# Branch B's gates in seven-product pairs, and branch B's projection beside the mLSTM

## The chip, the cores and the metric

The kernel runs on one core of one Trainium2 chip. The metric is the device time in microseconds of one launch. Before the change it is 1658.83 us, the median of 3 runs (1658.51 to 1659.03).

## The reference

One layer of a block with two branches, over S = 1024 positions and D = 1024 channels, in fp32. Both branches and both gates are cut out of one projection of the normed input; the branches are projected, gated, added, projected once more and added to the input.

```
h = rmsnorm(x, norm_g)
(a_q, a_k, a_v, a_o, a_z, a_g, b_q, b_k, b_v, b_z, g_a, g_b) = split(h @ w_in)
y_a = rmsnorm(mlstm(silu(conv(a_q, a_k)), a_v, a_g)) * sigmoid(a_o) * silu(a_z)   # both directions, 4 heads
y_b = rmsnorm(diff_attention(rope(b_q), rope(b_k), b_v)) * silu(b_z)              # 8 heads
mix = sigmoid(g_a + gate_b[0]) * (y_a @ w_branch_a) + sigmoid(g_b + gate_b[1]) * (y_b @ w_branch_b)
out = rmsnorm(x + mix @ w_out, final_g)
```

## The kernel before

All products run in fp32 by parts: each operand is split into a high part H and a low part L (`fp32r` tiles), and a product is three matmuls, wH·rH, wH·rL and wL·rH. A weight block of 1024×128 is loaded as `raw` (512 KB), cast to wH by ACT (L231) and subtracted to wL by POOL (L239, or in eight slices at L237). A projection of 128 outputs (`proj`, L565, matmuls L579) is two halves of 512 positions, each 8 blocks of k × 3 = 24 matmuls of 128x512; it is given out in eight pieces of three.

The stages, by the profile: an opening with norm and transposes; two wide pairs for a_v; sixteen pairs (a_k, a_q with their convolution, a_o, a_z) in which two blocks of 128 outputs together take seven half-size products in place of eight (`pair_units`, L355), 7×12 = 84 matmuls of 128x512 where two plain projections take 96; the differential attention, head by head; the mLSTM; the mixing; the output.

A pair's sink turns its sums into results and writes them to DRAM (`oz_sink`, L462; `conv_sink`, L492). The last product of a result stays in PSUM and one to three earlier ones come out of SBUF copies, so a sink gets a PSUM tile and a `rest` to add.

The sixteen gate projections (eight of g_b, then eight of g_a; `gate_units`, L984) are plain projections with a tanh on ACT (L993) and a store of the result. They are the *other work* that fills PE between dependent steps: five run in the attention's last part, eleven in the mLSTM, where `ml_units` (L1411) deals out their pieces by a table (`share`): three pieces before this step, two after that one.

After the mLSTM the mixing reads y_b from DRAM row by row (`load_y`, L1484: load of 512 KB into `yraw`, cast L1488 on ACT, subtraction L1489 on DVE), and multiplies: first a group of three units in step with the arriving rows (`first_units`, matmuls L1506), then five plain units for branch B, then eight for branch A, with y_a read in the meantime. Each unit's sum is gated out of PSUM by DVE (L1544), branch A's is added to branch B's (L1545), halved on ACT (L1547) and split for the last product (L1548). The w_out rows are loaded by `load_wo` (L1560; cast L1572, subtraction L1573).

Who sets the order: the `Weaver` (L70) writes PE's order out by hand. The other engines' queues are ordered by the tile scheduler, with exceptions: SP's is by hand from the last two gate units to the end of the group (`keep(E.PE, E.SP)`). All queues run in order. Nearly every DMA is issued by SP, and each of its DMAs also waits until the one eight before it has landed. Pools: h, the normed input's four tiles of 16 KB per partition, lives until the last gate projection, after which a pool `wr` takes its place.

## Time and profile before

The profiled execution took 1657.96 us, of which its span, from the first to the last instruction, is 1656.1 us. The stages of the span by the profile's windows (busy us of an engine within the stretch, granted clock of TensorE, share of time in which the DMA engines were busy):

| stretch, us | what | length | PE busy | DVE | ACT | POOL | clock | DMA |
|---|---|---|---|---|---|---|---|---|
| 0–66 | opening | 66 | 55.2 | 48.4 | 41.0 | 32.0 | 1.00 | 0.44 |
| 66–137 | wide pairs | 71 | 70.7 | 27.5 | 26.5 | 37.5 | 1.00 | 0.44 |
| 137–475 | sixteen pairs | 338 | 332.8 | 247.4 | 176.4 | 221.0 | 1.00 | 0.43 |
| 475–1112 | attention | 637 | 634.7 | 422.9 | 304.6 | 252.5 | 1.00 | 0.26 |
| 1112–1387 | mLSTM | 275 | 269.5 | 162.4 | 154.5 | 71.4 | 1.00 | 0.68 |
| 1387–1475 | group and branch B | 88 | 88.0 | 28.3 | 23.7 | 19.3 | 1.00 | 0.56 |
| 1475–1561 | branch A | 86 | 86.0 | 49.4 | 24.0 | 16.0 | 1.00 | 0.37 |
| 1561–1656 | output | 95 | 87.9 | 33.7 | 18.3 | 4.4 | 0.98 | 0.25 |

Durations are those of single instructions; matmuls are pipelined, so a matmul row's own length is longer than the distance to the next one, and PE's use is read from how many start in a stretch. In the timeline a row with `x2` stands for two instructions. SPq and ACTq rows are DMA issues and semaphore waits of these queues. An instruction that waits delays everything behind it in its queue.

### The profile page before, as it was taken

What the parts mean: (1) busy time and instruction counts of PE and PEld (TensorE: products, weight loads), DVE (VectorE), ACT (ScalarE), POOL (GpSimd) and SP (SyncE); (2) the same over time, 40 slices, a digit from 0 to 9 for tenths busy, and PEclk for the clock granted to TensorE, in tenths of its full rate; (3) what the DMA queues carried; (4) which work ended last, traced back from release to release, by engine and by line L of the source; (5) the groups of instructions that cost most, each with busy time, mean ns of one, the idle gap of its engine ahead of it and who ended that gap; (6) DMA issues with size and microseconds to landing.
All of it is one profiled execution on the core that took longest, in us unless ns stands there. A gap on an engine that the chain in (4) does not pass through costs nothing. (4 is left out here: it accounts for less than half of the span.)

```text
span 1656.1 us, 25333 instructions
## 1 busy us (share of the span) xinstructions
PE 1624.8 (98%) x9335; PEld 1371.3 (83%) x9335; DVE 1019.7 (62%) x1829; ACT 769.0 (46%) x1547; POOL 654.0 (39%) x700
## 2 busy tenths in 40 slices
PE   7999999999999999999999999999999999999998
PEld 6898778878779888889888888888988888888887
DVE  5733787696754776776677677624666663245533
ACT  6433555555533554554454545534566654132221
POOL 3744676767653551534435243133232221222000
PEclk9999999999999999999999999999999999999999
DMA  5433444344442322213132222128877537553222
GB/s 187 148 128 130 123 136 141 115 140 127 128 144 72 79 59 72 65 46 84 46 89 58 58 58 70 53 84 282 272 208 207 176 104 256 169 166 91 75 101 78
DMA packets 189711, 199.76 MB, mean 121 GB/s; under 512 B 11930, under 2 KB 143347, under 8 KB 189587
## 3 DMA queue, kind: packets, MB, share of 16 engines
q1 hardware_dynamic: 187090, 193.67, 38.8%
q10 hardware_dynamic: 2496, 4.47, 0.7%
q8 instruction: 74, 1.21, 0.3%
q14 instruction: 51, 0.41, 0.1%
HBM read 124.60 MB, written 56.72 MB: 109 GB/s over the span
## 5 line engine op out<-in xcount | busy, mean ns | idle before, releaser
L579 PE MATMUL pj<-hH,wH 128*128 128x512 f32 x640 | 261.3, 408 | 0.1
L579 PE MATMUL pj<-hH,wL 128*128 128x512 f32 x640 | 251.4, 393 | 0.8 <-POOL wL L237 0.8
L579 PE MATMUL pj<-hL,wH 128*128 128x512 f32 x640 | 250.6, 391 | 0.6 <-DVE hL L735 0.6
L1101 DVE TENSOR_REDUCE nm<-S 128x1 f32<-128x1024 f32 x128 | 150.7, 1219 | 108.8 <-PE S L1098 108.7
L239 POOL TENSOR_TENSOR wL<-raw,wH 128x1024 fp32r<-128x1024 f32 x34 | 85.0, 2501 | 173.4 <-ACT wH L231 171.0
L1103 ACT ACTIVATE e<-S,nm 128x1024 f32<-128x1024 f32 x128 | 142.7, 1130 | 7.0 <-DVE nm L1101 7.0
L579 PEld LDWEIGHTS pj<-hH,wL 128*128 128x128 f32 x640 | 120.1, 188 | 28.0 <-POOL wL L237 2.1
L579 PEld LDWEIGHTS pj<-hL,wH 128*128 128x128 f32 x640 | 120.7, 189 | 20.3 <-DVE hL L735 1.5
L1122 ACT CAST pH<-T 128x512 fp32r<-128x512 f32 x128 | 68.9, 589 | 147.6 <-PE T L152 147.6
L579 PEld LDWEIGHTS pj<-hH,wH 128*128 128x128 f32 x640 | 120.8, 189 | 19.1 <-ACT hH L734 0.5
L1098 PE MATMUL S<-kst,qq 64*128 64x512 f32 x768 | 106.2, 408 | 0.0
L1109 DVE SCALAR_TENSOR_TENSOR e<-e,r,e 128x1024 f32<-128x1024 f32 x64 | 93.5, 1460 | 1.8
L231 ACT CAST wH<-raw 128x1024 fp32r<-128x1024 f32 x47 | 49.5, 1053 | 94.4 <-PE pj L579 68.6
L1098 PEld LDWEIGHTS S<-kst,qq 64*128 64x128 f32 x768 | 67.3, 184 | 29.2 <-issue 9.4
L579 PE MATMUL pj<-sl_yb,wH 128*128 128x512 f32 x288 | 88.7, 389 | 0.0
L376 PE MATMUL T<-TH,wH 128*128 128x512 f32 x256 | 85.6, 394 | 2.3 <-ACT u L383 2.3
L523 DVE SCALAR_TENSOR_TENSOR pj<-cin,cols,pj 128x512 f32<-128x512 f32 x128 | 86.9, 746 | 0.0
L376 PE MATMUL T<-TH,wL 128*128 128x512 f32 x256 | 85.3, 394 | 1.6 <-ACT u L383 1.6
L1123 DVE TENSOR_TENSOR pL<-T,pH 128x512 fp32r<-128x512 f32 x128 | 82.0, 680 | 5.9 <-ACT pH L1122 5.9
L217 POOL TENSOR_TENSOR wL<-raw,wH 128x512 fp32r<-128x512 f32 x32 | 47.0, 1486 | 77.7 <-ACT wH L216 72.3
L152 PEld LDWEIGHTS T<-ident,e 128*128 128x128 f32 x512 | 54.9, 141 | 23.8 <-issue 23.7
L601 PE MATMUL pj<-wH,hH 128*128 128x256 f32 x256 | 74.3, 290 | 0.0
(409 smaller groups left out, 4455.0 us busy)
## 6 DMA issues: line engine op xcount, KB each, us to landing
raw<-in_w_in_dram SPq DMA_DIRECT2D x84, 512.0 KB, 4.0
kst<-hl SPq DMA_DIRECT2D x64, 128.0 KB, 2.4
qq<-hl SPq DMA_DIRECT2D x64, 128.0 KB, 2.4
x<-in_x_dram SPq DMA_DIRECT2D x8, 512.0 KB, 5.6
avH<-tz SPq DMA_DIRECT2D x16, 256.0 KB, 2.0
cak<-y SPq DMA_DIRECT2D x16, 256.0 KB, 2.6
cakH<-cin SPq DMA_DIRECT2D x16, 256.0 KB, 4.6
cakL<-tz SPq DMA_DIRECT2D x16, 256.0 KB, 4.4
```

The lines of the kernel that those rows point to most:

```text
L152: self.t.transpose(out, in_, self.ident[0:k, 0:k])
L239: self.p.tensor_tensor(out=wL, in0=raw, in1=wHf, op=ALU.subtract)
L376: self.t.matmul(ps, lhsT=l[:, k, :], rhs=r[:, k, :], start=(first and k == 0 and m == 0), stop=(k == 3 and m == 2), skip_group_check=not f ...
L523: v.scalar_tensor_tensor(out=acc, in0=raw[:, o + x:o + x + 512], scalar=w(x), in1=acc, op0=ALU.mult, op1=ALU.add)
L579: self.t.matmul(ps, lhsT=l[:, k, :], rhs=r, start=(n == 0), stop=(n == 23))
L601: self.t.matmul(ps[:, i, :], lhsT=l, rhs=r[:, k, :], start=(kh == 0 and k == 0 and m == 0), stop=(kh == 1 and k == 3 and m == 2))
L1098: self.t.matmul(ps[:, o], lhsT=qq[r, x, c], rhs=k[r, y, o], start=(m == 0), stop=(m == 2))
L1101: v.tensor_reduce(out=nm, in_=ps, axis=AX.X, op=ALU.max, negate=True)
L1103: a.activation(out=e, in_=ps, func=AF.Exp, bias=nm[:, 0:1], accum_out=Z[:, j, t:t + 1])
L1109: v.scalar_tensor_tensor(out=e0, in0=e, scalar=r[:, 0:1], in1=e0, op0=ALU.mult, op1=ALU.add)
L1122: a.copy(pH[:, :, s], ps)
L1123: v.tensor_tensor(out=pL[:, :, s], in0=ps, in1=pH[:, :, s].bitcast(F32), op=ALU.subtract)
```

## The change

Three parts hang together. First, the eight g_b projections leave the other work and become four more pairs after the sixteen, with a sink of their own (`gate_sink`). Second, in the attention and the mLSTM the other work is now the eight g_a projections, and behind them branch B's projection without its gate (`b_units`), whose results go to DRAM (`bd`). When the first of these pieces comes, at piece 48 of the mLSTM's other work, in the first head, h is given up, a pool `yb` takes its place, and all eight y_b rows are loaded into it (`load_b`), split by half rows: ACT casts, DVE subtracts. The last two gate units are reordered half by half, and the h tiles now stand half by half too. Third, the mixing is branch A alone. The group of three works on y_a; per unit the gate of A, the gate of B and branch B's sum are loaded (`mix_loads`, three times 512 KB), B is gated on DVE (`mix_b`), and each half is finished as before (`mix_a`). The y_a loads come where those of y_b stood, and the w_out rows have slots of their own, with two raw buffers in place of four.

```
+    def gate_sink(self, i0):
+        def sink(i, j, ps, rest):
+            if rest is not None:
+                to = self.psA.tile([128, 512], F32, name="pj", tag="pj", bufs=2) if i == j == 1 else ps
+                self.v.tensor_tensor(out=to, in0=ps, in1=rest, op=ALU.add)
+                ps = to
+            th = self.s0.tile([128, 512], F32, name="tz", tag="tz", bufs=2)
+            self.a.activation(out=th, in_=ps, func=AF.Tanh, scale=0.5, bias=self.gbh[:, 8 + i0 + i:9 + i0 + i])
+            self.q.dma_start(out=self.tg["gb"][i0 + i][:, j * 512:(j + 1) * 512], in_=th)
+        return sink
...
+    def halved(self, h, l):
+        for c in (slice(0, 512), slice(512, 1024)):
+            self.a.copy(h[:, c], l[:, c].bitcast(F32))
+            self.v.tensor_tensor(out=l[:, c], in0=l[:, c].bitcast(F32), in1=h[:, c].bitcast(F32), op=ALU.subtract)
+
+    def load_b(self, k, st):
+        h, l = (self.wb.tile([128, S], F32R, name=f"yb{x}", tag="yb", bufs=16) for x in "HL")
+        self.q.dma_start(out=l.bitcast(F32), in_=self.yb[k])
+        self.halved(h, l)
+        st["yb", k] = h, l
+
+    def b_units(self, i, st):
+        def done(half, ps):
+            t = self.wpool.tile([128, 512], F32, name="gt", tag="gt")
+            self.a.copy(t, ps)
+            (self.a if self.late else self.q).dma_start(out=self.bd[i][:, half * 512:(half + 1) * 512], in_=t)
...
+    def mix_b(self, i, st):
+        t = st["m", i]
+        for c in (slice(0, 512), slice(512, 1024)):
+            self.v.scalar_tensor_tensor(out=t["bm"][:, c], in0=t["tgb"][:, c], scalar=1.0, in1=t["bm"][:, c], op0=ALU.add, op1=ALU.mult)
+
+    def mix_a(self, i, half, ps, st):
...
+        v.scalar_tensor_tensor(out=t, in0=t, scalar=1.0, in1=ps, op0=ALU.add, op1=ALU.mult)
+        v.tensor_tensor(out=m, in0=m, in1=t, op=ALU.add)
+        self.a.mul(H[:, c], m, 0.5)
+        v.scalar_tensor_tensor(out=Lo[:, c], in0=m, scalar=0.5, in1=H[:, c].bitcast(F32), op0=ALU.mult, op1=ALU.subtract)
...
+            for n in range(0, 8, 2):
+                self.pairs.append((("gb", n), ("gb", n + 1)))
+                sinks.append(self.gate_sink(n))
...
-            gq = [("gb", i) for i in range(8)] + [("ga", i) for i in range(8)]
+            gq = [("ga", i) for i in range(8)]
...
-            rest = fill(len(gq))
+            rest, k = fill(len(gq)), self.PIECES
+            x, y = rest[-4 * k:-2 * k], rest[-2 * k:]
+            rest[-4 * k:] = x[:k] + y[:k] + x[k:] + y[k:]
+            swap = [leave("h"), enter("yb", "wb")] + [do(lambda k=k: self.load_b(k, st3)) for k in range(8)]
+            passB = sum((self.b_units(i, st3) for i in range(8)), [])
+            k = self.PIECES // 2
+            passB[:4 * k] = passB[:k] + passB[2 * k:3 * k] + passB[k:2 * k] + passB[3 * k:4 * k]
+            first = passB[0].fn
+            passB[0].fn = lambda: ([u.fn() for u in swap], first())
+            rest += passB
...
-            w.add(*loads[:4], wb(1), *rest[5:12], wb(2), *loads[4:], *rest[12:], do(lambda: setattr(self, "hold", False)))
+            w.add(*loads[:3], wb(1), *rest[5:12], wb(2), *loads[3:6], *rest[12:], *loads[6:], do(lambda: setattr(self, "hold", False)))
```

How the queues stand now. SP's queue at the swap, in the mLSTM's first head. Before (akf, akH, akL, aqH, aqL, vH, vL and gb are the head's operands from DRAM, tgb7 a gate's result, raw a block of weights):

```order
L1213 DMA akf_12646<-cak2_108 128x512
L1218 DMA aqH_12320<-caqH1_119 128x512
L994 DMA tgb7_81<-gt_12115 128x512
L1218 DMA aqL_12321<-caqL1_123 128x512
L194 DMA raw_12640<-in_w_in_dram 128x8x128
L1222 DMA gb_12423<-gg_2485 128x2x256
L1213 DMA akf_12771<-cak2_108 128x512
```

The same place after, with the y_b rows ybL:

```order
L1225 DMA akf_13274<-cak2_116 128x512
L1505 DMA ybL_12781<-yb0_90 128x1024
L1230 DMA aqH_12949<-caqH1_127 128x512
L1006 DMA tga7_73<-gt_12683 128x512
L1230 DMA aqL_12950<-caqL1_131 128x512
L1505 DMA ybL_12788<-yb1_91 128x1024
L194 DMA raw_13268<-in_w_branch_b_dram 128x8x128
L1505 DMA ybL_12795<-yb2_92 128x1024
L1234 DMA gb_13049<-gg_2493 128x2x256
L1225 DMA akf_13399<-cak2_116 128x512
L1505 DMA ybL_12802<-yb3_93 128x1024
L1505 DMA ybL_12809<-yb4_94 128x1024
```

The first four y_b loads are dealt out among the head's own loads, one behind each akf, aqL and raw; the second akf, which PE's transposes of the earlier akf release, stands ahead of the fourth.

SP's queue at the group's start, after (sl_yb are now the y_a rows, yraw the w_out rows, raw a block of w_branch_a):

```order
L1524 DMA sl_yb_15757<-ya0_82 128x1024
L1600 DMA yraw_16161<-in_w_out_dram 128x1024
L1600 DMA yraw_16243<-in_w_out_dram 128x1024
L1524 DMA sl_yb_15764<-ya1_83 128x1024
L1600 DMA yraw_16335<-in_w_out_dram 128x1024
L1524 DMA sl_yb_15771<-ya2_84 128x1024
L194 DMA raw_15808<-in_w_branch_a_dram 128x8x128
L1600 DMA yraw_16483<-in_w_out_dram 128x1024
L1524 DMA sl_yb_15813<-ya3_85 128x1024
L1600 DMA yraw_16491<-in_w_out_dram 128x1024
```

Where before the eight yraw loads of y_b stood by themselves with one block of weights among them, five w_out rows now stand between the y_a rows.

ACT's queue at the group's start, after (L1603 casts a w_out row, L1499 a y_a row, L1513 copies branch B's last half and L1514 stores it, L231 casts weights):

```order
L1499 CAST sl_yb_15756<-sl_yb_15757 128x512 x2
L1603 CAST sl_wo_16162<-yraw_16161 128x512
L1513 COPY gt_15845<-pj_15793 128x512
L1603 CAST sl_wo_16162<-yraw_16161 128x512
L1514 DMA bd7_113<-gt_15845 128x512
L1603 CAST sl_wo_16244<-yraw_16243 128x512 x2
L1499 CAST sl_yb_15763<-sl_yb_15764 128x512 x2
L1603 CAST sl_wo_16336<-yraw_16335 128x512 x2
L1499 CAST sl_yb_15770<-sl_yb_15771 128x512 x2
L231 CAST wH_15806<-raw_15808 128x1024
```

Before, the y_b casts followed each other here, with the third unit's weights after the fourth of them; now y_a rows 1 and 2 and these weights come behind the w_out rows.

ACT's queue at the group's end, after (L1554 is the halving of mix_a, bm the sum that it halves, wH_16026 the fourth unit's weights):

```order
L1499 CAST sl_yb_15848<-sl_yb_15849 128x512 x2
L1499 CAST sl_yb_15855<-sl_yb_15856 128x512 x2
L1554 ACTIVATE sl_r_16013<-bm_15870 128x512 x2
L1554 ACTIVATE sl_r_16037<-bm_15876 128x512 x2
L231 CAST wH_16026<-raw_16028 128x1024
L231 CAST wH_16050<-raw_16032 128x1024
L1554 ACTIVATE sl_r_16071<-sl_r_15882 128x512 x2
L231 CAST wH_16095<-raw_16054 128x1024
```

Before, no halving stood in this part, and the weight casts followed the casts of the y rows directly.

More of the change, by code (lines that the diff above doesn't have):

```diff
@@ new lines, in load_b @@
+    def load_b(self, k, st):
[8 more added lines that the diff above has]
+            (self.a if self.late else self.q).dma_start(out=self.bd[i][:, half * 512:(half + 1) * 512], in_=t)
+        un = []
+        for half in range(2):
+            c = slice(half * 512, (half + 1) * 512)
+            un += self.proj(("w_branch_b", 128 * i), half, lambda ps, half=half: done(half, ps),
+                            lambda k, c=c: (st["yb", k][0][:, c], st["yb", k][1][:, c]))
+        return un
@@ L1507, in piece @@
             if k == 7:
[L1508 to L1517 removed]
+                self.mix_a(i, half, ps, st)
+        un = [Unit(0.0, lambda: [self.mix_loads(i, st) for i in range(GROUP)]),
+              Unit(0.0, lambda: [self.mix_b(i, st) for i in range(GROUP)])]
         for step in range(8 + 2):
@@ L1566, in load_wo @@
         else:
-            raw = self.wy.tile([128, D], F32, name="yraw", tag="yraw", bufs=4)
+            raw = self.wy.tile([128, D], F32, name="yraw", tag="yraw", bufs=2)
             h, l = self.slot(which), self.slot(which)
```

101 lines of the change are left out of this document (35 added, 66 removed).

## The prediction

> **What bounds the kernel now.** First the page: the span, the busy time of each engine, the granted clock and the costliest groups.
>
> ```profile
> span 1656.1 us, 25333 instructions
> PE 1624.8 (98%) x9335; PEld 1371.3 (83%) x9335; DVE 1019.7 (62%) x1829; ACT 769.0 (46%) x1547; POOL 654.0 (39%) x700
> PEclk9999999999999999999999999999999999999999
> L239 POOL TENSOR_TENSOR wL<-raw,wH 128x1024 fp32r<-128x1024 f32 x34 | 85.0, 2501 | 173.4 <-ACT wH L231 171.0
> L231 ACT CAST wH<-raw 128x1024 fp32r<-128x1024 f32 x47 | 49.5, 1053 | 94.4 <-PE pj L579 68.6
> ```
>
> PE is busy 98% of the span, so the end is set by how many matmuls there are and how seldom PE stands still. Next the windows over the stages that the change touches (PE, PEld, DVE, ACT, POOL busy us, clock, DMA share, GB/s): two stretches of seven-product pairs, the mLSTM around the place of the swap, branch B, and the end.
>
> ```profile
> 240.00:260.00 20.00, 20.00 (x90) 16.57 (x89) 9.54 (x12) 8.65 (x15) 12.34 (x10) 1.00 0.34 98
> 400.00:420.00 20.00, 20.00 (x90) 16.55 (x89) 9.60 (x13) 8.08 (x14) 12.24 (x10) 1.00 0.34 97
> 1160.00:1180.00 20.00, 20.00 (x133) 17.97 (x132) 11.43 (x46) 11.27 (x27) 3.19 (x11) 1.00 0.99 322
> 1180.00:1200.00 20.00, 20.00 (x140) 18.41 (x139) 14.01 (x54) 11.71 (x31) 5.54 (x16) 1.00 0.74 219
> 1440.00:1480.00 40.00, 40.00 (x178) 33.12 (x177) 13.19 (x15) 10.47 (x13) 9.56 (x4) 1.00 0.41 132
> 1640.00:1656.00 16.00, 8.89 (x62) 8.14 (x60) 5.46 (x17) 3.19 (x8) 0.54 (x2) 0.86 0.17 67
> ```
>
> At 1440 there are 178 matmuls of 512 columns in 40 us, 0.225 us each, without a wait: that is the price of a removed one. At 1160 the DMA engines are busy 0.99 of the time. The profiled execution took 1657.96 us, 0.87 below the median of 1658.83; I make the sum as a difference and add it to the median.
>
> **Part 1, the four gate pairs: −10.8 us.** A pair costs 7×12 = 84 matmuls in place of 8×12 = 96, so four save 48: 48 × 0.225 = 10.8 us. This is on the path, since PE never runs dry there. The cover is the room of the other engines: a pair lasts 84 × 0.225 = 18.9 us, and the quoted pair stretches fill POOL 12.3 of 20, DVE 9.6 and ACT 8.7. A gate pair has the same loads and forms; its sink is an addition and four tanh, for which the groups further down show 0.69 us each. If POOL or the weights came late, the bound is the whole 10.8. I take nothing off.
>
> **Part 2, the swap in the mLSTM: +9.8 us.** At piece 48 of the other work PE needs y_b for the first time. Its next four pieces use rows 0 to 3, three matmuls each. The timeline of PE before, at the place of these four pieces (the third and fourth after the transposes of akf):
>
> ```profile
> 1181.89 0.39 PE L579 MATMUL pj<-hH,wH 128*128 128x512 f32 x1
> 1182.12 0.40 PE L579 MATMUL pj<-hL,wH 128*128 128x512 f32 x1
> ...
> 1182.82 0.39 PE L579 MATMUL pj<-hL,wH 128*128 128x512 f32 x1
> ...
> 1183.49 0.60 PE L152 MATMUL T<-ident,akf 128*128 128x128 f32 x4
> 1183.85 0.48 PE L579 MATMUL pj<-hH,wH 128*128 128x512 f32 x1
> 1184.16 0.40 PE L579 MATMUL pj<-hL,wH 128*128 128x512 f32 x1
> ...
> 1184.87 0.39 PE L579 MATMUL pj<-hL,wH 128*128 128x512 f32 x1
> ```
>
> Each piece needs the split row by its second matmul: 1182.12, 1182.82, 1184.16, 1184.87. The timeline of SP's queue at the same place shows when it gets to them:
>
> ```profile
> 1174.35 0.87 SPq L1230 DMA_DIRECT2D vH<-avH  x1
> ...
> 1177.06 0.65 SPq L1213 DMA_DIRECT2D akf<-cak  x1
> 1179.09 0.32 SPq L1218 DMA_DIRECT2D aqH<-caqH  x1
> 1180.36 0.38 SPq L1218 DMA_DIRECT2D aqL<-caqL  x1
> 1183.07 0.38 SPq L194 DMA_DIRECT2D raw<-in_w_in_dram  x1
> 1184.68 0.43 SPq L1213 DMA_DIRECT2D akf<-cak  x1
> ```
>
> By the order of after, row 0 stands behind the first akf (so 1177.7 to 1179.1, I take 1178.5), row 1 behind aqL, row 2 behind raw, row 3 behind the second akf. For what comes behind the issue: landing times near this place, then near 1363 to 1400, and the groups of a half-row cast and a half-row subtraction (min/median/max ns).
>
> ```profile
> raw<-in_w_in_dram SPq DMA_DIRECT2D x2, 512.0 KB, 8.2
> vH<-avH SPq DMA_DIRECT2D x2, 256.0 KB, 6.9
> ```
>
> ```profile
> yraw<-yb SPq DMA_DIRECT2D x8, 512.0 KB, 3.9
> raw<-in_w_branch_b_dram SPq DMA_DIRECT2D x3, 512.0 KB, 6.9
> ```
>
> ```profile
> L1572 ACT CAST sl_yb<-yraw x6: 616/620/622, 1475.5 to 1480.5; 128x512 fp32r<-128x512 f32 x6
> L1573 DVE TENSOR_TENSOR sl_yb<-yraw,sl_yb x6: 680/688/2273, 1476.2 to 1481.2; 128x512 fp32r<-128x512 f32 x6
> ```
>
> A row's first half is ready 0.62 + 0.69 = 1.3 us after landing. A 512 KB row lands in 3.9 to 8.2 us; for the first rows I take 5.4, midway between 3.9 and 6.9, for a queue that is busy but holds small transfers too. Row 0: 1178.5 + 5.4 + 1.3 = 1185.2, late by 3.1. Row 1 is issued when the load eight before it (vH, 1174.35 + 6.9 = 1181.3) has landed: 1181.3 + 5.4 + 1.3 = 1188.0, late by 5.2. Row 2: 1183.5 + 6.7 = 1190.2, late by 6.0. Row 3 is the dear one: the akf ahead of it on SP overwrites a buffer that PE's transposes read, and those stand behind row 1's piece on PE. They end at 1183.85 + 5.2 = 1189.05, the akf issues, row 3 starts at 1189.5; by then the queue has stood still, so it lands in 3.9: 1189.5 + 3.9 + 1.3 = 1194.7 against 1184.87, late by **9.8**. The late times don't add; the last one counts. With 3.9 for both landings it is 8.3, with 8.2 for both 16.9. Queued behind the waiting PE are the mLSTM's own S, I and state products, so nothing runs past it. Rows 4 to 7 are issued behind row 3 and first used after four more pieces with the second halves of rows 0 to 3.
>
> The 16 casts (9.9 us) and 16 subtractions (11.0) go on engines that are busy 11.7 and 14.0 of 20 us at 1180; with 9.8 us of standstill they fit (21.6 and 25.0 of 29.8), so I add nothing. PE shows no idle there that could be won back. The ungated results cost a copy and a store per half in place of a tanh and a store: the same.
>
> Between row 2's piece and row 3's, PE stands still for about 3.4 us. In the quoted windows the clock is 1.00, whatever the work, except at the end, with PE busy 8.89 of 16 us, where it is 0.86. By the row I add nothing. The Trainium skill's page "TensorE: Matmul & The Clock Gate" (Part 1) says that an idle window of about 3.4 us halves the clock until PE has been busy about as long again; by that page, as an estimate, up to 1.7 us more, 1668 in all.
>
> **Part 3, the mixing: +4.1 and +4.0 us.** The rows here are the group's first and last matmuls, the tanh ahead of it, the next unit and its weights, before:
>
> ```profile
> 1387.30 0.62 PE L1506 MATMUL T<-sl_yb,wH 128*128 128x512 f32 x2
> ```
>
> ```profile
> 1387.50 0.69 ACT L993 ACTIVATE gt<-pj,gbh 128x512 f32<-128x512 f32 x1 [2.35 <-PE pj L579]
> ```
>
> ```profile
> 1419.71 0.39 PE L1506 MATMUL T<-sl_yb,wL 128*128 128x512 f32 x1
> 1419.94 0.62 PE L579 MATMUL pj<-sl_yb,wH 128*128 128x512 f32 x2
> ```
>
> ```profile
> 1414.52 1.05 ACT L231 CAST wH<-raw 128x1024 fp32r<-128x1024 f32 x1 [4.64 <-PE T L1506]
> ```
>
> Before, PE goes through both seams without a wait: next start 0.23 us on. After, three w_out loads stand ahead of y_a row 2. ACT: the copy of the last half of branch B ends at about 1388.1, a half cast of the first w_out row 1388.75, the store's issue and two casts of the second 1390.3, y_a row 1 at 1390.9. The third w_out load waits for the first one's subtraction, about 1389.5, and y_a row 2 is issued behind it at 1389.9, its neighbour w_branch_a behind that at 1390.3. The weights land in 3.9 to 6.9 (5.0: two transfers wait), their cast (1.05) stands behind row 2's halves at 1396.4 and POOL's L239 takes 2.5: ready at 1400.0. PE needs them with the third unit's third matmul: group start 1387.3, 12 pieces of 0.68, and 0.45: 1395.9. Late by **4.1**; by 6.2 with a landing of 8.2, by 3 if the casts fall better.
>
> At the group's end ACT has the four half multiplications of units 0 and 1 ahead of the cast of the fourth unit's weights; each waits for DVE's chain. The same operations before:
>
> ```profile
> L1544 DVE SCALAR_TENSOR_TENSOR tgl<-tgl,pj x16: 676/687/689, 1481.8 to 1561.7; 128x512 f32<-128x512 f32 x16
> L1545 DVE TENSOR_TENSOR sl_mb<-sl_mb,tgl x16: 683/691/693, 1482.5 to 1562.4; 128x512 f32<-128x512 f32 x16
> L1547 ACT ACTIVATE sl_r<-sl_mb x8: 632/632/634, 1483.2 to 1519.5; 128x512 fp32r<-128x512 f32 x8
> ```
>
> From the end of unit 0 DVE has ten such operations to the last addition of unit 1: four of unit 0, then two for unit 1's sums, two for its gated branch B and two additions. The last six can't start before unit 1's own end, two pieces of 0.68 later: 1.4 + 6 × 0.69 = 5.5 at least, 10 × 0.69 = 6.9 with no overlap; I take 5.7. Then a multiplication (0.63), the cast (1.05) and L239 (2.5): +9.9. PE is through with units 1 and 2 at 24 × 0.225 = +5.4 and needs the low weights at +5.9. Late by **4.0**; 5.2 by the longer chain, 2 if DVE's operations overlap, since then only the cast and L239 count. The remaining five units have all of this ahead of them, and the tail is unchanged.
>
> **The sum.** −10.8 + 9.8 + 4.1 + 4.0 = +7.1: 1658.83 + 7.1 = **1666 us**, slower. Its own range: 1661 (8.3, 3 and 2) to 1671 (13, 5 and 5).
>
> **The rivals.** *A, the loads are in time* (faster): y_b has lain in memory since the attention, SP gets to row 0 before PE does, and the seams' waits hide behind the mLSTM's and group's own work. It decides at a landing plus split of under 3 us at the swap. Time: 1658.83 − 10.8 = 1648, with one short wait 1652. For it: the DMA share falls to 0.74 at 1180. Against: no 512 KB row is below 3.9. Chance 0.18. *B, it cancels*: row 3 is not held by the transposes, so the swap costs one landing (5 us), and only one seam waits (4): −10.8 + 9 = −1.8, 1657. Chance 0.17. *C, a crowded queue*: both landings 8.2: −10.8 + 16.9 + 8.1 = +14.2, 1673. For it: 0.99 at 1160. Against: PE's standstill empties the queue. Chance 0.11. *D, the pairs don't give their 48 matmuls back*, because POOL falls behind: up to 10.8 more than the forecast, 1677. Against: POOL 12.3 of 20. Chance 0.04.
>
> **How the numbers follow.** The forecast keeps 0.50. 0.2% is 3.3 us, about what a measurement of this kernel can tell from no change. Faster: A and 0.05 of B, 0.23. Within: 0.12 of B. Slower: 0.50 + 0.11 + 0.04 = 0.65. A range from 1650 to 1673 leaves out half of A and half of C with D, under 2 in 10.
>
> **What would show it.** In the profile after: 48 fewer matmuls and the mLSTM's start 10.8 us earlier (part 1); near piece 48 a wait of PE for DVE's ybL, of 8 to 17 us in all, the longest at row 3, with ACT's cast released by the DMA; at the group's third unit a wait for POOL's wL, and another at the fourth unit, with ACT's cast behind the multiplications. If PE's waits there are under 3 us in all, or if the mLSTM makes its delay good further on, the prediction is wrong.

## The result, and the profile after

The changed kernel takes 1681.43 us (median of 4 runs, 1679.68 to 1682.56), the kernel before 1658.67 beside it: a ratio of 1.0135, 95% interval 1.0121 to 1.0150. That is 22.8 us slower, where 7.1 were forecast; 1681 lies above the range. The profiled execution took 1680.89 us. Of all the runs below one was disturbed, early_rows: two of its four executions, the profiled one among them, took 2658.03 and 4094.26 us and are left out. The page of after:

```profile
span 1679.1 us, 25444 instructions
...
PE 1626.1 (97%) x9287; PEld 1367.1 (81%) x9287; DVE 1037.8 (62%) x1869; ACT 792.9 (47%) x1611; POOL 678.3 (40%) x724
...
PEclk9999999999999999999999999999997999999999
```

There are 48 matmuls fewer (9335 to 9287), and yet the span is 23.0 us longer than 1656.1. One slice of the clock row shows a 7 where before there were only nines. The lengths of the stages, each from its first matmul in the timeline to the next stage's (b is a plain unit of 48 matmuls, 10.88 us by the spacing of matmuls in both kernels; the 87.04 of the first row are eight times that):

| stage | before, us | after, us | difference, with eight units b moved |
|---|---|---|---|
| gates in front (8 b less, four pairs more) | 87.04 | 75.56 | −11.5 |
| attention to the mLSTM's first state product | 630.4 | 631.7 | +1.3 |
| mLSTM up to the group | 243.8 | 265.1 | +21.3 |
| the group of three | 32.4 | 36.3 | +3.9 |
| gap between group and next unit | 0.2 | 2.1 | +1.9 |
| single units (13 before, 5 after) | 141.2 | 60.2 | +6.0 |
| output, to the end of the span | 94.7 | 94.7 | 0 |

Before rounding the sum is +23.0, the difference of the spans. So 21.3 of it arise in the mLSTM and 11.8 around the group, while the pairs give 11.5 back.

The windows of after (PE, PEld, DVE, ACT, POOL busy us, clock, DMA share, GB/s): a gate pair, the mLSTM just ahead of the swap, the swap, and the single units' start.

```profile
480.00:500.00 20.00, 20.00 (x90) 16.57 (x89) 6.35 (x8) 9.09 (x16) 11.07 (x10) 1.00 0.52 152
1240.00:1260.00 20.00, 18.19 (x129) 16.63 (x127) 12.38 (x44) 10.84 (x25) 9.92 (x22) 1.00 0.98 296
1260.00:1265.00 5.00, 1.73 (x3) 0.69 (x3) 2.40 (x8) 2.30 (x5) 0.29 (x1) 0.81 1.07 391
1270.00:1275.00 5.00, 1.95 (x3) 0.79 (x3) 2.17 (x4) 1.50 (x4) 0.00 (x0) 0.50 0.64 174
1280.00:1285.00 5.00, 5.00 (x29) 4.98 (x29) 3.47 (x12) 1.44 (x5) 0.50 (x3) 0.64 0.40 128
1285.00:1290.00 5.00, 4.70 (x30) 3.97 (x28) 3.10 (x10) 3.32 (x8) 0.40 (x1) 1.00 0.91 292
...
1528.00:1532.00 4.00, 3.84 (x9) 3.07 (x10) 4.00 (x3) 1.16 (x2) 2.89 (x2) 0.50 0.65 218
```

The gate pair runs as the pairs before it, 90 matmuls in 20 us. At the swap PE starts three matmuls in five microseconds; the granted clock is 0.81 in that window and 0.50 in the one from 1270 to 1275. What PE waits for in the mLSTM (us in total, times, longest), and when the pieces with rows 0 to 3 begin:

```profile
PE pj L591 <- ACT ybH L1499: 11.7, 4, 4.9
```

```profile
1262.62 0.50 PE L591 MATMUL pj<-ybH,wH 128*128 128x512 f32 x1 [3.88 <-ACT ybH L1499]
...
1265.81 0.80 PE L591 MATMUL pj<-ybH,wH 128*128 128x512 f32 x1 [1.24 <-ACT ybH L1499]
...
1270.66 0.80 PE L591 MATMUL pj<-ybH,wH 128*128 128x512 f32 x1 [1.63 <-ACT ybH L1499]
...
1277.52 0.80 PE L591 MATMUL pj<-ybH,wH 128*128 128x512 f32 x1 [4.91 <-ACT ybH L1499]
...
1282.05 0.42 PE L148 MATMUL T<-vL,kwH 128*128 128x258 f32 x1
1282.27 0.42 PE L148 MATMUL T<-vH,kwL 128*128 128x258 f32 x1
...
1284.07 0.28 PE L148 MATMUL SS<-akH,aqH 128*128 128x256 f32 x1
1284.19 0.28 PE L148 MATMUL SS<-akL,aqH 128*128 128x256 f32 x1
```

Each of the four pieces waits for the cast of its row. Small products that follow start 0.22 us apart at 1282 and 0.12 apart at 1284: half speed up to there. The low clock began at about 1263, right behind the first wait, by the 0.81 of the window from 1260. SP's queue at this place:

```profile
1254.93 0.32 SPq L1505 DMA_DIRECT2D ybL<-yb  x1
...
1258.26 0.52 SPq L1505 DMA_DIRECT2D ybL<-yb  x1
...
1260.16 1.18 SPq L1505 DMA_DIRECT2D ybL<-yb  x1
1268.74 0.37 SPq L1234 DMA_DIRECT2D gb<-gg  x1
1269.20 0.42 SPq L1225 DMA_DIRECT2D akf<-cak  x1
1269.67 0.90 SPq L1505 DMA_DIRECT2D ybL<-yb  x2
```

Rows 0, 1 and 2 go out within 5.2 us. Then the queue stands until 1268.74 in front of gb, and row 3 leaves at 1269.67 behind gb and akf. What ends that standstill is to be seen on POOL, and the end of row 3's trip on ACT:

```profile
1268.31 0.40 POOL L1317 TENSOR_SCALAR_AFFINE_SELECT W<-gb 128x256 f32<-128x256 f32 x1 [4.40 <-PE T L152]
```

```profile
1261.95 0.62 ACT L1499 CAST ybH<-ybL 128x512 fp32r<-128x512 f32 x1 [3.96 <-DMA ybL<-yb]
...
1265.13 1.14 ACT L1499 CAST ybH<-ybL 128x512 fp32r<-128x512 f32 x2 [0.78 <-DMA ybL<-yb]
...
1276.85 2.38 ACT L1499 CAST ybH<-ybL 128x512 fp32r<-128x512 f32 x4 [5.35 <-DMA ybL<-yb]
```

The last reader of the earlier gb is this POOL instruction; it ends at 1268.71, and gb goes out 0.03 us later. POOL had waited 4.40 us for PE's transposes of W, which stand behind row 1's late piece. PE's transposes of akf follow them and end at 1269.03, and the akf's load goes out at 1269.20. So gb holds row 3 back hardly at all; the akf does. Row 3, issued at 1269.67, is cast at 1276.85, 7.2 us later. The landing times of the stretch:

```profile
ybL<-yb SPq DMA_DIRECT2D x8, 512.0 KB, 6.9
```

In the group, its third unit's weights and PE's wait for them:

```profile
1495.39 2.39 POOL L239 TENSOR_TENSOR wL<-raw,wH 128x1024 fp32r<-128x1024 f32 x1 [17.31 <-ACT wH L231]
```

```profile
1497.83 0.51 PE L1567 MATMUL T<-sl_yb,wL 128*128 128x512 f32 x1 [0.46 <-POOL wL L239]
```

Behind the group, what PE waits for, and ACT, POOL and DVE between the group and the single units:

```profile
PE pj L591 <- POOL wL L239: 3.5, 1, 3.5
PE pj L591 <- ACT wH L231: 1.7, 1, 1.7
```

```profile
1521.72 1.23 ACT L1554 ACTIVATE sl_r<-bm 128x512 fp32r<-128x512 f32 x2 [2.37 <-DVE bm L1553]
1522.86 1.98 ACT L231 CAST wH<-raw 128x1024 fp32r<-128x1024 f32 x2
```

```profile
1523.96 6.92 POOL L239 TENSOR_TENSOR wL<-raw,wH 128x1024 fp32r<-128x1024 f32 x2 [26.19 <-ACT wH L231]
1533.25 2.40 POOL L239 TENSOR_TENSOR wL<-raw,wH 128x1024 fp32r<-128x1024 f32 x1 [2.36 <-ACT wH L231]
```

```profile
1525.82 1.27 DVE L1552 SCALAR_TENSOR_TENSOR sl_r<-sl_r,T 128x512 f32<-128x512 f32 x2
1527.02 4.42 DVE L1553 TENSOR_TENSOR sl_r<-sl_r 128x512 f32<-128x512 f32 x2
...
1533.35 3.45 DVE L1544 SCALAR_TENSOR_TENSOR bm<-tgb,bm 128x512 f32<-128x512 f32 x2 [0.52 <-DMA bm<-bd]
```

As forecast, the cast stands behind the halvings and each halving behind DVE. But the subtraction, 2.40 us in the single one at 1533.25, takes 6.92 for two here, and two of DVE's additions take 4.42 where the two gatings of A ahead of them (L1552) take 1.27.

### The profile page after: what moved, and what is told of

The parts are those of the page before. It is cut to its first block, busy times and chain, and to the rows that moved or that the text cites. A ratio compares the mean times of both kernels' runs of the same rounds, so it can differ in the third digit from the quotient of the medians.

```text
span 1679.1 us, 25444 instructions
## 1 busy us (share of the span) xinstructions
PE 1626.1 (97%) x9287; PEld 1367.1 (81%) x9287; DVE 1037.8 (62%) x1869; ACT 792.9 (47%) x1611; POOL 678.3 (40%) x724
## 4 chain that ended last, share of the span: by engine, by line
PE 63%; DVE 5%; DMA 3%; issue 3%; ACT 3%; POOL 1%; SPq 0%; POOLq 0%; ACTq 0%; DVEq 0%
PE pj L591 23%; PE T L376 9%; PE T L1146 5%; PE S L1110 5%; PE T L152 5%; PE pj L613 5%; PE pj L1633 5%; PE I L148 2%; PE T L148 2%; DMA ybL<-yb 1%; PE T L1567 1%; PE SS L148 1%; PE PO L148 1%; DMA raw<-in_w_in_dram 1%; POOL wL L239 0%
## 5 line engine op out<-in xcount | busy, mean ns | idle before, releaser
L591 PE MATMUL pj<-hH,wH 128*128 128x512 f32 x512 | 208.2, 407 | 0.1
L591 PE MATMUL pj<-hH,wL 128*128 128x512 f32 x512 | 201.1, 393 | 0.8 <-POOL wL L237 0.8
L591 PE MATMUL pj<-hL,wH 128*128 128x512 f32 x512 | 200.3, 391 | 0.6 <-DVE hL L747 0.6
L591 PEld LDWEIGHTS pj<-hH,wL 128*128 128x128 f32 x512 | 96.1, 188 | 22.6 <-POOL wL L237 2.2
L239 POOL TENSOR_TENSOR wL<-raw,wH 128x1024 fp32r<-128x1024 f32 x26 | 66.2, 2549 | 118.8 <-ACT wH L231 118.8
L591 PEld LDWEIGHTS pj<-hL,wH 128*128 128x128 f32 x512 | 96.5, 189 | 17.6 <-DVE hL L747 1.4
L591 PEld LDWEIGHTS pj<-hH,wH 128*128 128x128 f32 x512 | 96.4, 188 | 16.2 <-ACT hH L746 0.5
L376 PE MATMUL T<-TH,wH 128*128 128x512 f32 x320 | 106.8, 393 | 2.6 <-ACT u L383 2.6
L376 PE MATMUL T<-TH,wL 128*128 128x512 f32 x320 | 106.3, 393 | 1.6 <-ACT u L383 1.6
L376 PE MATMUL T<-hH,wL 128*128 128x512 f32 x240 | 79.6, 391 | 0.7 <-DVE oz L477 0.7
L376 PE MATMUL T<-hH,wH 128*128 128x512 f32 x240 | 79.0, 390 | 0.0
```

The lines of the kernel that those rows point to most:

```text
L376: self.t.matmul(ps, lhsT=l[:, k, :], rhs=r[:, k, :], start=(first and k == 0 and m == 0), stop=(k == 3 and m == 2), skip_group_check=not f ...
L591: self.t.matmul(ps, lhsT=l[:, k, :], rhs=r, start=(n == 0), stop=(n == 23))
```

## The experiments

Two theories to begin with. *Lateness*: the y_b rows come late at the swap, because they are asked for late and land in 7 us, and nothing else in the mLSTM is wrong; rows loaded in time bring the 21.3 us down to little. *Work*: the loads, casts, subtractions and stores of branch B crowd the mLSTM wherever they stand, and an earlier load moves the loss. For the group: a wait for SP's order, and behind it a chain of weights against a queue of DVE. All runs in one table (medians; ratio to the kernel before with its interval; lengths as in the stage table; early_rows has no usable trace):

| run | us | ratio | mLSTM | group | gap | five units |
|---|---|---|---|---|---|---|
| before | 1658.67 | | 243.8 | 32.4 | 0.2 | 54.4 (by 10.88) |
| after | 1681.43 | 1.0135 [1.0121, 1.0150] | 265.1 | 36.3 | 2.1 | 60.2 |
| sp_by_hand | 1676.02 | 1.0107 [1.0092, 1.0122] | 264.1 | 32.4 | 2.1 | 60.1 |
| warm_pe | 1676.33 | 1.0113 [1.0098, 1.0129] | 263.1 | 37.2 | 2.1 | 60.9 |
| rows_on_act_queue | 1681.74 | 1.0143 [1.0127, 1.0160] | 265.4 | 36.1 | 2.1 | 60.9 |
| early_rows | 1669.51, 1670.33 | 1.007 [1.005, 1.009] | | | | |
| early_by_hand | 1669.01 | 1.0060 [1.0045, 1.0075] | 253.8 | 34.1 | 2.1 | 60.2 |
| spread_rows | 1668.70 | 1.0058 [1.0043, 1.0073] | 255.2 | 34.4 | 2.1 | 59.6 |
| load_then_split | 1663.39 | 1.0032 [1.0019, 1.0045] | 251.3 | 34.4 | 2.1 | 59.7 |
| store_from_act | 1664.75 | 1.0039 [1.0024, 1.0054] | 250.6 | 34.0 | 2.1 | 59.7 |
| no_split | 1661.13 | 1.0014 [1.0004, 1.0023] | 248.8 | 33.9 | 2.1 | 59.6 |
| no_split_own_stores | 1656.01 | 0.9984 [0.9975, 0.9993] | 243.8 | 32.4 | 2.1 | 59.7 |
| halve_dve | 1681.74 | 1.0140 [1.0123, 1.0157] | 267.9 | 36.0 | 0.2 | 62.9 |
| seam | 1678.61 | 1.0119 [1.0104, 1.0135] | 266.3 | 32.5 | 0.2 | 63.4 |
| weights_on_dve | 1676.12 | 1.0107 [1.0092, 1.0122] | 267.7 | 32.6 | 0.2 | 60.4 |
| all_four | 1669.20 | 1.0062 [1.0047, 1.0077] | 256.1 | 32.4 | 0.2 | 61.0 |
| spread_and_weights | 1667.73 | 1.0055 [1.0040, 1.0070] | 255.2 | 34.1 | 0.2 | 60.8 |
| store_and_seam | 1664.97 | 1.0043 [1.0028, 1.0058] | 251.0 | 33.1 | 0.2 | 63.3 |
| half_the_sums | 1681.03 | 1.0135 [1.0120, 1.0150] | 265.8 | 33.9 | 5.7 | 59.0 |
| load_then_split_half_the_sums | 1666.07 | 1.0048 [1.0032, 1.0065] | 250.9 | 34.0 | 5.7 | 58.2 |

The lengths are of one profiled execution each, which can lie some microseconds from the median (warm_pe's was its slowest, 1680.55). Where an edit leaves the mLSTM as it is in after, its length still runs from 264.1 to 267.9, so a difference of a few microseconds between two lengths shows nothing by itself. The runs no_split, no_split_own_stores, half_the_sums and load_then_split_half_the_sums leave out operations that the result needs: they show where time goes and are no versions to use.

**Rows asked for sooner.** The rows live in the h tiles themselves, whose two halves are free one after the other, and are loaded and split at piece 32 (rows 0 to 3) and 48 (rows 4 to 7) of the other work.

```
-        h, l = (self.wb.tile([128, S], F32R, name=f"yb{x}", tag="yb", bufs=16) for x in "HL")
+        h, l = (x[k // 4].rearrange("p k e -> p (k e)")[:, k % 4 * S:(k % 4 + 1) * S] for x in (self.hH, self.hL))
...
-            swap = [leave("h"), enter("yb", "wb")] + [do(lambda k=k: self.load_b(k, st3)) for k in range(8)]
+            early = rest[32].fn
+            rest[32].fn = lambda: ([self.load_b(k, st3) for k in range(4)], early())
+            swap = [do(lambda k=k: self.load_b(k, st3)) for k in range(4, 8)]
```

> The change with one difference: rows 0 to 3 of y_b are written into the half of h that comes free first, so their loads and splits are issued sixteen pieces earlier; rows 4 to 7 stay at the swap. Theory 1 (the loads): PE stands still at the swap because four loads, each about 7 us from issue to landing, are issued there one after another, the fourth behind PE's own transposes. Then 17 to 21 of the 21.3 us that the mLSTM grew by go: 1661 to 1664 us, and no wait of PE for a y_b cast above 1 us. Theory 2 (the splits): 16 casts on ACT and 16 subtractions on DVE delay the mLSTM's own steps; then the delay only moves sixteen pieces ahead: 1672 us or more, with PE's waits for W and kwH grown. Clock back at 1.00 there by theory 1.

It took 1669.51 and 1670.33, ratio 1.007 [1.005, 1.009]. 11 us came back, more than *work* and less than *lateness* allows: both hold in part.

**Keeping PE's clock up.** 50 matmuls with zero weights, 11.3 us at 0.225, go ahead of the first four branch-B pieces.

```
+            if key == ("w_branch_b", 0) and half == 0:
+                for e in range(self.extra.get(i, 0)):
+                    self.t.matmul(ps, lhsT=self.zero, rhs=wH[:, 0:4, :].rearrange("p k e -> p (k e)"), start=(i == e == 0), stop=False)
...
+            self.extra = {0: 16, 1: 6, 2: 8, 3: 20}
```

> The change with 50 matmuls of a zero weight added to the first block's sum (16, 6, 8 and 20 ahead of the first four pieces of branch B), so that PE works while it waits. If the half clock from 1262 to 1283 us costs time of its own, the stretch of 4.3 us from the fourth piece to the state products takes 2.4 and the pieces in the chain 0.2 to 0.4 less each: 3 to 4 us in all, 1677.5 to 1678.5, although 11.3 us of matmuls are added. If the clock only falls where PE waits anyway, the time stays at 1681 or grows by what the added matmuls overrun the waits (up to 3 us).

1676.33: with 11 us of useless matmuls added, it is 5 us faster than after. Two windows of it at the swap:

```profile
1265.00:1270.00 5.00, 4.26 (x19) 3.06 (x20) 3.25 (x10) 2.63 (x6) 0.70 (x2) 1.00 0.85 310
1270.00:1275.00 5.00, 5.00 (x23) 4.05 (x23) 3.90 (x7) 3.79 (x9) 0.00 (x0) 1.00 0.36 93
```

The clock is 1.00 where it was 0.50. So the half clock had a price of its own, about 5 us by the medians, with the added work already paid (by the one profile alone it would be 2.0 in the mLSTM).

**SP by hand to the end of the program.** In the change the order of SP's queue is written out up to the end of the group and left to the scheduler behind it, which moves loads of w_out up. Here it stays written out to the end, so y_a's loads don't stand behind those of w_out.

```
-            w.add(leave("yb"), enter("wr", "wr"), *group, keep(E.PE))
+            w.add(leave("yb"), enter("wr", "wr"), *group)
```

> The change with SP's queue kept in the written order to the program's end, so that no w_out load stands between the y_a loads. Theory 1 (the w_out rows in between): the group's 3.9 us of waits fall to under 1 us: about 1678. Theory 2 (the y_a rows and the third unit's weights themselves land too late after the mLSTM): waits of 3 us or more stay, 1680 to 1682.

1676.02; the group is 32.4 us long, as before the change. The +3.9 there came from the order of the loads. **Both together**, the rows early and SP by hand:

> Rows 0 to 3 of y_b sixteen pieces earlier, and SP in the written order to the end: both differences together. If they are independent: 1681.4 less 11.4 (early rows, at 1670) less 5.4 (1676.0 alone) = 1664.6. The trace shows what is left of the mLSTM's 21.3 us with the early rows. Theory 1 (the loads at the swap): no wait for rows 0 to 3, and what is left stands before piece 32, where SP waits for PE to free h, or at rows 4 to 7. Theory 2 (the splits): PE's waits for W and kwH have grown at pieces 32 to 40.

1669.01: no better than the rows alone at 1669.51 and 1670.33, where 1664.6 was expected if the two gains were independent; its group is 34.1 us, not 32.4. Its mLSTM is 253.8 us, 10.0 above that of before, though the rows are no longer late at the swap.

**The rows' issue on another queue**, ACT's instead of SP's (`self.a.dma_start` in `load_b`).

> The change with y_b's eight loads issued by ACT in place of SP, at the same place. If the 7 us from issue to landing come from the transfers queued ahead on SP's ring (the broadcast gb and akf), and the late issue from SP's waits, rows 0 to 3 land about 4 us after issue and the waits at the swap fall by half: 1671 to 1675. If the DMA engines themselves are full, landing stays at 7 and the time at 1679 to 1683.

1681.74, the same as after. The loads themselves went faster, by the median:

```profile
ybL<-yb ACTq DMA_DIRECT2D x8, 512.0 KB, 4.0
```

That is 4.0 us in place of 6.9, and still nothing is gained: each row's issue now stands in ACT's queue behind the cast of the row before. Rows 1, 2 and 3 go out at 1263.13, 1267.54 and 1271.55, in after at 1258.26, 1260.16 and 1269.67, and row 3's cast again begins 6.8 us behind its issue. PE waits 12.7 us in all for the casts, in after 11.7. Whether the landings are shorter because of the queue or because the rows come one after another isn't separated.

**One row at a time.** Loaded and split at pieces 32, 35, 38, 41, 44, 47, 50 and 52, SP by hand.

```
+            for k, i in enumerate((32, 35, 38, 41, 44, 47, 50, 52)):
+                rest[i].fn = lambda k=k, f=rest[i].fn: (self.load_b(k, st3), f())
```

> SP in the written order, and the eight y_b rows loaded and split one at a time, at pieces 32, 35, 38, 41, 44, 47, 50 and 52 in place of four and four. If the rest of the mLSTM's growth is the bursts of eight casts and eight subtractions, the mLSTM comes within 3 us of the kernel before (10 us at four and four): 1661 to 1664. If it is their sum of 21 us on ACT and DVE, or the DMA, however spread, 1667 to 1670.

1668.70: spreading alone gives nothing over 1669.01. In both, the rows' casts stand in ACT's queue right behind the loads. In the run with the rows early and SP by hand, one such cast:

```profile
1257.94 0.40 ACT L1319 ACTIVATE W<-W,gc_negM 128x128 f32<-128x128 f32 x1 [0.78 <-POOL W L1317]
1260.69 1.14 ACT L1499 CAST hH<-hL 128x512 fp32r<-128x512 f32 x2 [2.35 <-DMA hL<-yb]
1261.73 0.36 ACT L1379 CAST WH<-T 128x256 fp32r<-128x256 f32 x1
1262.00 0.51 ACT L1319 ACTIVATE W<-W,gc_negM 128x256 f32<-128x256 f32 x1
```

For 2.35 us ACT waits for a row of the second four, which PE needs only later, and the mLSTM's WH and W queue behind it. **The split put later than the load** tests this: loads at pieces 32 to 35, 42, 44, 46 and 48, splits at 40, 42, 44, 46, 49, 51, 53 and 54.

```
+            for k, (i, j) in enumerate(zip((32, 33, 34, 35, 42, 44, 46, 48), (40, 42, 44, 46, 49, 51, 53, 54))):
+                rest[i].fn = lambda k=k, f=rest[i].fn: (self.load_b(k, st3), f())
+                rest[j].fn = lambda k=k, f=rest[j].fn: (self.halved(*st3["yb", k]), f())
```

> SP in the written order, y_b's rows loaded early one by one (pieces 32 to 35, 42, 44, 46, 48) and each split only five to eleven pieces later (40, 42, 44, 46, 49, 51, 53, 54). Theory 1 (the casts stand in ACT's queue ahead of the mLSTM's own steps and wait there for their row to land): the waits of PE for W and kwH behind them go, and the mLSTM's growth falls from 10 us (rows early) to about 5, where leaving the splits out took it: 1662 to 1664. Theory 2 (the 21 us of casts and subtractions are too much for ACT and DVE): it stays at 10, 1667 to 1669.

1663.39, 5.6 us faster with the same instructions, moved. The loads' places changed along with the casts', so the casts' place is the likely cause but not the only difference, and the two profiled mLSTMs differ by 2.5 us only. The largest wait that is left in its mLSTM is the same fault once more, at the cast of row 0:

```profile
1228.99 0.62 ACT L1499 CAST hH<-hL 128x512 fp32r<-128x512 f32 x1 [4.41 <-DMA hL<-yb]
```

```profile
1230.03 0.39 PE L148 MATMUL T<-vH,kwH 128*128 128x258 f32 x1 [3.25 <-ACT kwH L1262]
```

ACT waits 4.41 us for the landing with the mLSTM's kwH behind the cast, and PE then waits 3.25 us for kwH. It is the fastest complete version, and still 0.32% slower than before.

**No split at all.** Early rows and SP by hand, the casts and subtractions of y_b left out.

```
-        self.halved(h, l)
-        st["yb", k] = h, l
+        st["yb", k] = l, l
```

> Rows 0 to 3 early and SP in the written order, as before, but the y_b rows aren't split: the 16 casts and 16 subtractions are left out, and the loaded row stands for both parts. If what is left of the mLSTM's growth (10 us over the kernel before, with waits of PE for kwH, WL and W) comes from the splits on ACT and DVE, 7 to 10 us go: 1659 to 1662. If it comes from the eight loads ahead of the mLSTM's own loads on SP, it stays at 1667 to 1670.

1661.13, mLSTM 248.8: without any split 5.0 us are left, by this one profile. The largest wait of PE in it, and ACT ahead of the W it waits for:

```profile
PE T L152 <- ACT W L1364: 4.2, 2, 3.5
```

```profile
1288.43 0.59 ACT L1512 COPY gt<-pj 128x512 f32<-128x512 f32 x1 [3.67 <-DMA bd<-gt]
```

ACT's copy of a finished half waits 3.67 us for the store of the half before it, since both use the single gt buffer. This wait comes with the early rows: in the change itself ACT's copies in the mLSTM wait for PE and for no store.

```profile
ACT gt L1513 <- PE pj L591: 10.8, 5, 4.2
```

**Stores issued by ACT** in `load_then_split`:

```
-            (self.a if self.late else self.q).dma_start(out=self.bd[i][:, half * 512:(half + 1) * 512], in_=t)
+            self.a.dma_start(out=self.bd[i][:, half * 512:(half + 1) * 512], in_=t)
```

> As load_then_split, and branch B's sums are stored from ACT's queue, as the tail does, in place of SP's. Theory: what was left without splits (5 us, nearly all in one wait of 3.9 us for W, with ACT standing at the copy of the second half until SP had stored the first) is the single buffer of these sums behind SP's queue; then another 3 to 5 us go: 1658 to 1661. If the copy waits for the transfer itself, and not for its issue, it stays.

1664.75, no gain: the copies there still wait for the landing of a store, 6.3 us in two places. **A buffer of its own for each of the sixteen halves**, in `no_split`, where the hH tiles are free:

```
-            t = self.wpool.tile([128, 512], F32, name="gt", tag="gt")
+            t = self.hH[i // 4].rearrange("p k e -> p (k e)")[:, (2 * (i % 4) + half) * 512:(2 * (i % 4) + half + 1) * 512]
```

> The kernel whose y_b rows are loaded early and not split (1661.13, mLSTM 248.8 us against 243.8 before the change), with a buffer of its own for each of the sixteen half results of branch B in place of the single one, so that ACT never waits for a store to land before it empties the next sum (the results are rounded on the way, and the output differs as it did there). Theory 'single buffer': the wait of ACT's copy for the store (3.67 us in one place there) holds the mLSTM's casts up and is most of the 5 us that are left: 1656.5 to 1658.5, mLSTM 245 or less. Rival: those waits are taken from slack, as when the stores went to ACT's queue: 1660.5 to 1661.5, mLSTM 248 to 249, and the 5 us are loads (y_b rows, weights) in the way of the mLSTM's own.

1656.01, and the mLSTM of its profile (its fastest execution, 1654.95) is 243.8 us, that of before to the tenth. PE's wait for W is down to

```profile
PE T L152 <- ACT W L1364: 0.8, 1, 0.8
```

So the mLSTM comes back to its length. Taken off in this order, it gives 11.3 with the rows asked for sooner (265.1 to 253.8), 5.0 with the splits (to 248.8), 5.0 with the single store buffer (to 243.8). These are gains of one step on the last, not the parts of the changed kernel's 21.3: rows that come early bring waits of their own, as the store buffer shows.

**Behind the group: relieving ACT.** The halving of the first three units goes to DVE, so the weights' cast doesn't wait for it.

```
+        if i < GROUP:
+            v.tensor_scalar_mul(out=H[:, c], in0=m, scalar1=0.5)
+        else:
+            self.a.mul(H[:, c], m, 0.5)
```

> The change with the halving of the first three units on DVE in place of ACT, so that ACT can cast the fourth unit's weights at once. Theory 1 (the cast behind the halvings): the 7 to 8 us at the seam behind the group fall to 1 to 3: 1674.5 to 1676.5. Theory 2 (POOL's subtraction is slowed by a busy DVE, or the weights land late): 5 us or more stay, 1679 or above, with POOL's subtraction at 4 us.

1681.74. The gap is gone (0.2), but one unit later PE waits 5.9 us for DVE, which is busy 9.97 of 10 us there:

```profile
PE pj L591 <- DVE tga L1552: 5.9, 1, 5.9
```

```profile
1530.00:1540.00 10.00, 6.12 (x27) 4.72 (x26) 9.97 (x15) 0.00 (x0) 2.08 (x1) 1.00 0.87 292
```

**The gating of B moved forward on DVE** as well, ahead of the group's last step, with SP by hand:

```
+            group[1:39] = group[2:39] + [keep(E.PE, E.SP, E.DVE), group[1]]
```

> SP in the written order to the end, the first three units' halving on DVE, and the gating of their branch B sums on DVE ahead of the group's last step (DVE in the written order there). Theory 1 (DVE's queue behind the group is the bound, whoever halves; the cast behind the halvings only hides it): with six operations of it done earlier the whole wait at the seam goes, 8 us under the 1676.0 of the written order alone: 1668 to 1669. Theory 2 (POOL's subtraction beside a busy DVE): 3 us or more are left, 1671 or above.

1678.61, slower than SP by hand alone (1676.02): the gap is 0.2, the five units 63.4. **The late weights' subtraction on DVE** in place of POOL, gating forward, halving on ACT:

```
+                late = key[0] == "w_branch_a" and key[1] >= 128 * GROUP
+                (self.v if late else self.p).tensor_tensor(out=wL, in0=raw, in1=wHf, op=ALU.subtract)
```

> SP in the written order, the gating of the group's branch B sums on DVE ahead of the last step, ACT halving as in the change, and the weight subtractions of the last five units on DVE in place of POOL. Theory 1 (POOL and DVE slow each other behind the group: 2.4 us become 4.1 there, and DVE's pairs of 1.3 become 4.4): 1.9 + 5.8 us of the 1676.0 of the written order alone go, 1668 to 1670, although DVE gets 1.2 us more for each unit. Theory 2 (DVE's queue alone is too long behind the group): the added subtractions make it longer, 1675 or above.

1676.12, as SP by hand alone (1676.02): PE now waits 3.1 us for DVE's wL. **The combinations**: early rows, SP by hand, halving and gating; then the rows one at a time with the weights on DVE; then `store_from_act` with the gating forward.

> The early rows, SP in the written order, the halving on DVE and the gating ahead of the last step, together. Sum of the parts: 1664.6 less 8 = 1656 to 1657, within 0.2% of the kernel before; 1648 would need the mLSTM to lose all of its 21 us.

1669.20, ratio 1.0062 [1.0047, 1.0077].

> The spread rows, SP in the written order, the gating ahead of the last step and the weight subtractions on DVE, together. If both theories 1 hold: 1661 to 1664 less 7 = 1654 to 1657, a little under the kernel before (1658.6). If only one holds, 1661 or above.

1667.73, 1.0055 [1.0040, 1.0070].

> As store_from_act, and the group's gating on DVE ahead of its last step, ACT halving, POOL subtracting the weights. If the casts of the next weights then come ahead of the halvings, and DVE's queue is six operations shorter, the 7.7 us behind the group fall to 2 to 4: 1653 to 1657, under the kernel before (1658.6). If POOL and DVE still slow each other there, 1658 or above.

1664.97, 1.0043 [1.0028, 1.0058], with 6.4 us of waits for DVE's gating. In none of them does relief behind the group reach the total: in all_four gap and group are shorter than in early_by_hand by 1.9 and 1.7 us, but the mLSTM, which these edits don't touch, is 2.3 longer in the profiled execution, and the five units 0.8. Why isn't shown.

**Half of DVE's sums left out** in the group, 12 of its 24 operations there, everything else as in `sp_by_hand`:

```
-              Unit(0.0, lambda: [self.mix_b(i, st) for i in range(GROUP)])]
...
+        if i < GROUP:
+            m = t
+        else:
+            v.tensor_tensor(out=m, in0=m, in1=t, op=ALU.add)
```

> The change with SP's queue by hand up to the group's end (1676.02), and in the group's three units branch B and its gate are left out of the sum: no gating of B and no addition there, so DVE has 12 operations fewer between the group and the next unit, 12 in place of 24, and the output lacks branch B in three of eight blocks. Loads, products, casts and weights are the same. Theory 'DVE's queue': what PE loses behind the group, about 8 us (2.1 between the group and the next unit, 5.7 in the five units over their 54.4), is DVE's length of queue, whoever of the others is relieved. Then most of it goes: 1668 to 1671, the gap between group and next unit under 1 us and the five units under 57. Theory 'weights': the fourth unit's weights are late because their cast and subtraction have to be done after the group, with or without DVE: 1674 to 1676, the gap still 2.

1681.03 against 1676.02: *slower* than with those operations in. By the lengths, gap and units grew by 2.5 us (64.7 against 62.2); the rest lies in the mLSTM, which the edit doesn't touch, and the group, which it touches only by the gating; their lengths differ by as much between other runs. ACT's queue and POOL in it:

```profile
1524.15 0.63 ACT L1557 ACTIVATE sl_r<-sl_r 128x512 fp32r<-128x512 f32 x1 [2.98 <-DVE sl_r L1552]
1524.69 1.98 ACT L231 CAST wH<-raw 128x1024 fp32r<-128x1024 f32 x2
```

```profile
1525.80 4.68 POOL L239 TENSOR_TENSOR wL<-raw,wH 128x1024 fp32r<-128x1024 f32 x2 [31.04 <-ACT wH L231]
```

With shorter sums the scheduler puts the weights' cast behind all six halvings in place of four, and PE waits 5.3 us for it. So the theory that the length of DVE's queue is the whole loss falls: with 12 operations fewer the loss grew, and the cast's place in ACT's queue counts too. What each costs by itself this run doesn't show, since the halvings ahead of the cast still wait for DVE (2.98 us before the last one). The two subtractions, without DVE beside them, take 2.34 us each. The same in `load_then_split`:

> The same leaving out (no B and no gate of B in the group's three units) in the kernel that loads the rows early and splits them later (1663.39). If the wait behind the group is DVE's alone and has nothing to do with the mLSTM, the two add: 1663.4 less 5 to 8, 1656 to 1658, no slower than before the change (1658.7). If a part of it comes back elsewhere: 1660 to 1663.

1666.07, ratio 1.0048 [1.0032, 1.0065], with a gap of 5.7 as well: slower than with the sums, again with the cast behind the halvings.

## Why the prediction was wrong

*Direction and places* were right: slower, with waits at rows 0 to 3, at the group's start and at the fourth unit's weights. Two of four sizes were wrong.

*The four pairs*, −10.8: they measured −11.5. The gate pairs run without waits.

*The swap*, +9.8, is where it failed: the mLSTM grew by 21.3. PE's products come in the same order in both kernels, so their lateness can be followed through the trace. Measured from the last product ahead of the swap, the second matmul of row 3's piece, on which the prediction set its 9.8, is 16.7 us late; when the products are back at full pace it is 19.2, and at the group's start 21.5 (0.2 were gained ahead of the swap).

The first step that failed is the landing. The prediction took 5.4 us for the first rows and said of row 3 "by then the queue has stood still, so it lands in 3.9". Rows 0 to 2 landed in 7.0, 6.9 and 7.6, and row 3 was cast 7.2 after its issue. With 7 us for all, the prediction's own chain gives 14.5 in place of 9.8. The chain was right: row 3 stood behind the akf, the akf behind PE's transposes, and the last late time counted.

The second step is "I add nothing" for the clock; the 1.7 us by the page fell short too. The waits of 3.88, 1.24, 1.63 and 4.91 us let the clock fall to 0.50. The transposes that release row 3 then ran at half speed: from row 1's piece to their end it takes 3.2 us, before 1.5. That is most of the way from 14.5 to 16.7, and the 2.5 us from row 3's piece to full pace come on top. The Trainium skill's page "TensorE: Matmul & The Clock Gate" (Part 1) asks for a stretch of sustained work before the clock comes back. The trace agrees, with a longer stretch than the 3.4 us that the prediction quotes: after the last wait PE worked from 1277.52 without a pause, and the products are at full pace at about 1283.6, 6 us later. What I missed is that four waits in a row keep PE from such a stretch, so that the low clock lasted from about 1263 to 1283.6 and not for one window. `warm_pe` puts the price at about 5 us.

"They fit, so I add nothing", of 16 casts and 16 subtractions, and "the same", of the ungated copy and store, compared busy times. In the changed kernel what they cost behind the swap can't be more than the 2.3 us from full pace to the group. They failed in earnest once the rows came early. The casts fit into ACT's time, but not into its order: each waits for its landing at the head of a queue that the mLSTM needs (in `load_then_split` 4.41 us in one place, with kwH behind it). And the copy's single buffer is held until the store has landed, which cost about 5 us in `no_split`.

*The group's start*, +4.1: measured 3.9. The size held, and so did its reason, the loads of w_out ahead of y_a's and the weights' (`sp_by_hand`). The place was partly another: the third unit's weights were ready at 1497.8, 12.3 us after the group's start where 12.7 were forecast, but PE had already stood for y_a's rows and waited only 0.46 for them. So the match in size is partly luck.

*The fourth unit's weights*, +4.0: measured 7.9, the gap's 1.9 and the units' 6.0. The chain was the forecast one, DVE, halving, cast, subtraction. The weights were ready 12.0 us after unit 0's end in place of 9.9; the cast began nearly as forecast (6.8 against 6.3). So the last link was mis-sized, 2.5 us from a row in which DVE was less busy, against 4.1 for the first subtraction here, and the clock was at 0.50 in the 4 us behind the waits (9 matmuls from 1528 to 1532 in place of 18, some 2 us). The Trainium skill's page "SBUF — State Buffer" (section "Who interferes with whom") says that a VectorE instruction with two SBUF inputs and a GpSimd instruction that reads SBUF exclude each other. The trace agrees: the additions with two SBUF inputs take 4.42 us for two beside L239, the gatings with one input in PSUM 1.27, and L239 is at 2.34 when DVE is idle (`half_the_sums`). Which side is held up differs: the first subtraction takes 4.14 us beside two gatings of B (L1544, two SBUF inputs) that take 1.28, and the one at 1533.25 takes 2.40 beside two that take 3.45.

*The rivals.* C, a crowded queue, came nearest, with 1673. Its 16.9 at the swap meet the 16.7 of row 3's piece partly by luck, from landings of 8.2 where about 7 were measured and with no half clock in the chain, and it has nothing for the 4.8 us behind that. The sign that the prediction gave, a wait of PE for DVE's ybL, didn't come either: PE waited 11.7 us for ACT's ybH, one step ahead of it in the chain.

What stays open: whether the 7.9 us behind the group come back if the cast's place and DVE's queue are relieved at once. Each run relieved at most a part: in `seam` and `store_and_seam` the wait for the cast is gone (gap 0.2), and PE then waits 5.9 and 6.4 us for DVE. What makes up the 2.3 us between full pace and the group isn't shown. A complete kernel with more than one store buffer wasn't tried, nor `load_then_split` with only the casts moved. The attention's +1.3 lies in the 630.6 to 632.5 that it takes in the other runs, whose edits don't touch it.

## What to carry to other kernels

Work that is moved beside a dependent chain must be fitted into each engine's order, not only into its idle time: a load's first consumer goes into an in-order queue where the load has landed, not where it is issued. A buffer that was enough has to be counted again when a change moves loads beside its stores; here that showed only once the rows came early. A wait that forms in a chain of short steps is paid twice if TensorE's clock falls during it, so several short waits in a row are priced with the clock of the whole stretch.
